# Attention scores as two products over all 128 rows, with tokens stored so that position classes are runs of 16 words

## The chip, the core and the metric

The kernel runs on one core of a Trainium2 chip. The core has five engines with instruction queues of their own: TensorE (PE, matrix products; its weight loads are listed apart as PEld), VectorE (DVE), ScalarE (ACT), GpSimd (POOL) and SyncE (SP, which here issues every DMA). The metric is the device time of one execution in microseconds (us); lower is better. The kernel before takes 2600.39 us, the median of 3 runs (2598.51 to 2601.74).

## What is computed

One encoder layer runs over two independent streams: a prompt of 1024 tokens and a sample of 512, 1024 channels each, all in float32. Per stream:

```
u = rmsnorm(x) @ w_in
ssd_out = ssd_mixer(...)                       # scan over chunks, both directions
att_out = attention_mixer(u_q, u_k, u_v, ...)  # 8 heads of 64 channels
h = x + concat(ssd_out, att_out) @ w_out
h = h + memory_cross_attention(rmsnorm(h), rmsnorm(mem), ...)
y = h + square(relu(rmsnorm(h) @ w1)) @ w2
```

The change is in `attention_mixer`. Queries and keys are normed and rotated, and then

```
for window, dil in ((128, 1), (512, 4), (2048, 16)):
    o, lse = band_pattern(q, k, v, dil, window // (2 * dil))
w = softmax(stack(lses)); out = sum(w * stack(outs))
```

Each pattern lets a query see the keys of its own class of positions modulo `dil`, at most 64 steps of that class away. All three together are one softmax over the union, with keys that are counted twice where two patterns hold them.

## The kernel before, in words

Precision. TensorE multiplies rounded float32 words (F32R). A number is split into a rounded part (hi) and the exact rest (lo), and a product of two such numbers is three products: hi·hi, hi·lo and lo·hi (`mm3`, L171 to L174). These are most of TensorE's work. Weights are loaded as `raw` by SP, rounded by ScalarE into `whi`, and the rest `wlo` is made by GpSimd or VectorE (`load_w`, L153 to L165; `raw` has two buffers).

Stages. The input projection writes its parts to DRAM: `heads` (L411 on) norms and rotates queries and keys, transposes them on TensorE (L423, with the unit matrix `ident`) and stores them as `qk`, rounded part and rest, tokens along the row. Values are stored as `vd` token by token (L442). The scan (`ssd`), the attention (`att`), the memory's keys and values, `w_out`, the cross attention and the MLP follow.

Attention. `att` runs `att_pair` for four pairs of heads. `att_load` (L575) loads a pair's operands: per head `aq` holds the rounded queries (64 rows) above their rests (64 rows), `ak` the rounded keys twice above each other, and `akl` the rests of both heads' keys. There is one buffer of each, so a pair waits for the pair before it. The work goes in units of two tiles of 128 queries of one head. First come the band units (neighbouring positions), then the class units (positions modulo 4, for the two dilated patterns). In a class unit the operands are read from the same tiles with a step of four: `q[:, r:T:4]` and `k[:, 64 + r:64 + T:4]`. The scores of one tile are two products into PSUM bank `ma`:

```
nc.tensor.matmul(pq[:, i, :W], q(qA[h]), k(kB[h]), start=True, stop=False)        # L638
nc.tensor.matmul(pq[:, i, :W], q(qA[h][rs]), k(kC[rs]), start=False, stop=True)   # L639
```

L638 goes over 128 rows (hi·hi + lo·hi) and L639 over the 64 rows of one head (hi·lo). W, the number of keys, is 256, and 128 in the class units of the sample. VectorE adds the mask and takes the maximum (L641), ScalarE takes the exponential (L646), TensorE transposes the result (L652, bank `mb`), VectorE or ScalarE copies it to `apT`, and TensorE multiplies it by the values (L662, bank `mc`; `avb` for the band, `avc` for classes). The results of a class unit go through DRAM (`ncl`) back into token order and are merged with those of the band. At the end `mix_T` (L753) loads both mixers' results and transposes them with `to_T` (L185).

The sample has 32 units (16 band, 16 class), the prompt 64 (32 and 32).

Order. The order of all instructions on each engine is made before the run by a scheduler that simulates the program's time; each engine then works through its list in that order. Products of the input projection, of the memory, of `w_out` and of the cross attention stand between the steps of an attention unit.

## Time and profile before

| what | value |
|---|---|
| median of 3 runs | 2600.39 us (2598.51 to 2601.74) |
| span of the profiled execution | 2603.1 us, the only time that the profile gives for that execution |
| TensorE busy | 2537.7 us, 97% |
| TensorE weight loads | 2328.8 us, 89% |
| VectorE busy | 1404.3 us, 54% |
| ScalarE busy | 954.7 us, 37% |
| GpSimd busy | 678.0 us, 26% |
| DMA | 269.36 MB, 103 GB/s on average |

A row of the timeline has the start of an instruction, how long it took, its engine and line, and what it wrote and read (the moving operand first, then the weights). TensorE's products are pipelined: their durations overlap, so what a product costs in a stream is the distance from its start to the next one's. "Idle before" is time in which the engine did nothing before an instruction, and the name behind it is what ended that time.

### The profile page before, as it was taken

What the parts mean: (1) busy time and instruction counts of PE and PEld (TensorE: products, weight loads), DVE (VectorE), ACT (ScalarE), POOL (GpSimd) and SP (SyncE); (2) the same over time, 40 slices, a digit from 0 to 9 for tenths busy, and PEclk for the clock granted to TensorE, in tenths of its full rate; (3) what the DMA queues carried; (4) which work ended last, traced back from release to release, by engine and by line L of the source; (5) the groups of instructions that cost most, each with busy time, mean ns of one, the idle gap of its engine ahead of it and who ended that gap; (6) DMA issues with size and microseconds to landing.
All of it is one profiled execution on the core that took longest, in us unless ns stands there. A gap on an engine that the chain in (4) does not pass through costs nothing.

```text
span 2603.1 us, 43137 instructions
## 1 busy us (share of the span) xinstructions
PE 2537.7 (97%) x17363; PEld 2328.8 (89%) x17363; DVE 1404.3 (54%) x2734; ACT 954.7 (37%) x2153; POOL 678.0 (26%) x476
## 2 busy tenths in 40 slices
PE   8989999899899999999999999999999999999999
PEld 8889999889888888788999999999899898999987
DVE  6895663787644454645544564544734434444344
ACT  5655443355544454443222232433522121212110
POOL 3362011565322121214333321111222122212211
PEclk9999999999999999989999999999999999999999
DMA  6755342656736242414322251111111111110101
GB/s 191 239 195 156 94 135 84 217 186 210 213 115 212 62 119 72 125 37 168 99 95 96 83 172 39 42 57 49 49 33 50 49 49 49 49 49 33 65 33 65
DMA packets 216054, 269.36 MB, mean 103 GB/s; under 512 B 26514, under 2 KB 171184, under 8 KB 215856
## 3 DMA queue, kind: packets, MB, share of 16 engines
q1 hardware_dynamic: 215856, 266.62, 32.1%
q8 instruction: 136, 2.23, 0.4%
q14 instruction: 62, 0.51, 0.1%
HBM read 212.37 MB, written 54.20 MB: 102 GB/s over the span
## 4 chain that ended last, share of the span: by engine, by line
PE 71%; DVE 4%; DMA 2%; ACT 1%; issue 1%; POOL 1%; SPq 0%; DVEq 0%; POOLq 0%; ACTq 0%
PE mm L172 13%; PE mm L174 13%; PE mm L173 13%; PE tp L174 7%; PE tp L173 7%; PE tp L172 7%; PE mc L662 2%; PE ma L639 2%; PE ma L638 2%; PE mb L652 1%; PE tp L190 1%; DMA se<-acp 1%; DVE wlo L164 1%; DVE se L545 1%; PE tp L801 0%
## 5 line engine op out<-in xcount | busy, mean ns | idle before, releaser
L172 PE MATMUL mm<-whi,chi 128*128 128x256 f32 x1792 | 517.6, 289 | 3.9 <-DVE h L779 2.0
L174 PE MATMUL mm<-whi,clo 128*128 128x256 f32 x1792 | 514.1, 289 | 2.3 <-DVE clo L196 2.3
L173 PE MATMUL mm<-wlo,chi 128*128 128x256 f32 x1792 | 514.3, 288 | 0.0
L926 DVE TENSOR_TENSOR h<-mm,h 128x512 f32<-128x512 f32 x384 | 261.9, 689 | 422.5 <-PE mm L174 422.5
L164 POOL TENSOR_TENSOR wlo<-raw,whi 128x1024 fp32r<-128x1024 f32 x120 | 294.2, 2452 | 697.7 <-ACT whi L163 693.4
L174 PE MATMUL tp<-chi,wlo 128*128 128x256 f32 x1440 | 409.3, 284 | 0.0
L173 PE MATMUL tp<-clo,whi 128*128 128x256 f32 x1440 | 408.4, 284 | 0.0
L172 PE MATMUL tp<-chi,whi 128*128 128x256 f32 x1440 | 406.1, 282 | 0.0
L163 ACT CAST whi<-raw 128x1024 fp32r<-128x1024 f32 x240 | 241.9, 1047 | 338.1 <-PE mm L174 208.6
L172 PEld LDWEIGHTS mm<-whi,chi 128*128 128x128 f32 x1792 | 342.6, 191 | 8.6 <-ACT mm L729 2.3
L173 PEld LDWEIGHTS mm<-wlo,chi 128*128 128x128 f32 x1792 | 342.4, 191 | 2.9 <-issue 0.9
L174 PEld LDWEIGHTS mm<-whi,clo 128*128 128x128 f32 x1792 | 340.8, 191 | 4.7 <-DVE clo L196 2.5
L164 DVE TENSOR_TENSOR wlo<-raw,whi 128x1024 fp32r<-128x1024 f32 x120 | 270.3, 2252 | 102.9 <-ACT whi L163 98.1
L172 PE MATMUL mm<-whi,hidh 128*128 128x512 f32 x768 | 303.1, 395 | 1.2 <-DVE h L926 1.2
L173 PE MATMUL mm<-wlo,hidh 128*128 128x512 f32 x768 | 302.5, 394 | 0.0
L174 PE MATMUL mm<-whi,hidl 128*128 128x512 f32 x768 | 302.0, 393 | 0.0
L172 PEld LDWEIGHTS tp<-chi,whi 128*128 128x128 f32 x1440 | 273.4, 190 | 9.4 <-issue 0.4
L174 PEld LDWEIGHTS tp<-chi,wlo 128*128 128x128 f32 x1440 | 272.5, 189 | 7.2
L173 PEld LDWEIGHTS tp<-clo,whi 128*128 128x128 f32 x1440 | 271.6, 189 | 6.6
L911 POOL TENSOR_TENSOR hidl<-hr,hidh 128x512 fp32r<-128x512 f32 x96 | 136.4, 1420 | 453.4 <-ACT hidh L910 453.4
L910 ACT CAST hidh<-hr 128x512 fp32r<-128x512 f32 x96 | 59.6, 621 | 326.4 <-PE mm L173 249.9
L174 PEld LDWEIGHTS mm<-whi,hidl 128*128 128x128 f32 x768 | 144.3, 188 | 33.6
(282 smaller groups left out, 4550.7 us busy)
## 6 DMA issues: line engine op xcount, KB each, us to landing
raw<-in_mlp_w_dram SPq DMA_DIRECT2D x128, 512.0 KB, 4.2
raw<-in_w_in_dram SPq DMA_DIRECT2D x48, 512.0 KB, 4.8
qkp<-ev SPq DMA_DIRECT2D x32, 256.0 KB, 3.1
se<-acp SPq DMA_DIRECT2D x16, 512.0 KB, 5.0
raw<-in_xatt_wkv_dram SPq DMA_DIRECT2D x16, 512.0 KB, 4.4
raw<-in_w_out_dram SPq DMA_DIRECT2D x16, 512.0 KB, 4.6
raw<-in_xatt_wq_dram SPq DMA_DIRECT2D x16, 512.0 KB, 4.6
raw<-in_xatt_wo_dram SPq DMA_DIRECT2D x16, 512.0 KB, 3.8
```

The costliest lines, as they stand in the source:

```text
L163: nc.scalar.copy(hi[:, sl, :], raw)
L164: (nc.vector if s else nc.gpsimd).tensor_tensor(lo[:, sl, :], raw, f(hi[:, sl, :]), op=OP.subtract)
L172: nc.tensor.matmul(ps, lh, rh, start=start, stop=False)
L173: nc.tensor.matmul(ps, lh, rl, start=False, stop=False)
L174: nc.tensor.matmul(ps, ll, rh, start=False, stop=stop)
L190: nc.tensor.transpose(pt[:, k, t, :], xn[t][:, (2 * kp + k) * 128:(2 * kp + k + 1) * 128], ident)
L638: nc.tensor.matmul(pq[:, i, :W], q(qA[h]), k(kB[h]), start=True, stop=False)
L639: nc.tensor.matmul(pq[:, i, :W], q(qA[h][rs]), k(kC[rs]), start=False, stop=True)
L662: nc.tensor.matmul(po[:, i * 64:i * 64 + 64], pT[:, i * nk + j, :], ops[i][2][j][:, rs], start=j == 0, stop=j == nk - 1)
L910: nc.scalar.copy(hh[:, ft], r)
L911: nc.gpsimd.tensor_tensor(hl[:, ft], r, f(hh[:, ft]), op=OP.subtract)
L926: nc.vector.tensor_tensor(h[t][:, cs], ps, h[t][:, cs], op=OP.add)
```

## The change

Tokens are stored in another order. Within each group of 64 tokens, the 16 of class 0 (modulo 4) come first, then those of class 1, 2 and 3. For queries and keys a permutation matrix `perm` takes the place of the unit matrix in the transpose of `heads`; values are stored in that order by four DMAs in place of one; the masks of the band are permuted likewise; and `mix_T` turns the attention's half of the channels back by transposing with `back`. A class is then read from the keys as runs of 16 words, and a class's queries are copied into a tile of their own (`qc`) by GpSimd.

`att_load` is split: `att_values` loads the values of a pair, and `att_head` the queries and keys of one head. Both key tiles now have the same keys in both halves: `k[0]` the rounded part twice, `k[1]` the rest twice. A tile's scores are two products over 128 rows with the same queries: (hi + lo)·hi and (hi + lo)·lo, so lo·lo is added to what was computed. A head's band units and class units come one after the other, then the second head. Keys and queries have three buffers each, and a head takes two of each.

```diff
@@ tables, constants
-T_BAND, T_CLP, T_CLS, T_ROPE = 256, 256 + 768, 256 + 768 + 512, 256 + 768 + 512 + 128
-T_END = T_ROPE + 128
+T_BAND, T_CLP, T_ROPE = 256, 256 + 704, 256 + 704 + 512
+T_PERM, T_BACK = T_ROPE + 128, T_ROPE + 256
+T_END = T_BACK + 128
...
+    tok = np.arange(64).reshape(16, 4).T.reshape(-1)
+    tok = (64 * np.arange(4)[:, None] + tok).reshape(-1)
+    t[tok[:128], T_PERM + np.arange(128)] = 1.0
+    t[np.arange(128), T_BACK + tok[:128]] = 1.0
...
+    perm, back = tab[:, T_PERM:T_PERM + 128], tab[:, T_BACK:T_BACK + 128]
@@ to_T
-                    nc.tensor.transpose(pt[:, k, t, :], xn[t][:, (2 * kp + k) * 128:(2 * kp + k + 1) * 128], ident)
+                    nc.tensor.transpose(pt[:, k, t, :], xn[t][:, (2 * kp + k) * 128:(2 * kp + k + 1) * 128],
+                                        units(2 * kp + k))
@@ heads, w_in_qkv
-                    nc.tensor.transpose(pt[:, o:o + 128], e[:, i, hp * 128:hp * 128 + 128], ident)
+                    nc.tensor.transpose(pt[:, o:o + 128], e[:, i, hp * 128:hp * 128 + 128], perm)
...
-                    dst = st.vd[64 + t * 128:64 + t * 128 + 256, (c - 4) * 256:(c - 3) * 256]
-                    nc.sync.dma_start(dst.rearrange("(t p) c -> p t c", p=128), e)
+                    for i in range(2):
+                        for g in range(2):
+                            r0 = 64 + (t + i) * 128 + g * 64
+                            dst = st.vd[r0:r0 + 64, (c - 4) * 256:(c - 3) * 256]
+                            nc.sync.dma_start(dst.rearrange("(r j) c -> j r c", r=4), e[g * 64:g * 64 + 64, i, :])
@@ att_load becomes att_values and att_head
-        qA = [pool.tile([128, T], F32R, name=f"aq{h}", bufs=1) for h in range(2)]
-        kB = [pool.tile([128, T + 128], F32R, name=f"ak{h}", bufs=1) for h in range(2)]
-        kC = pool.tile([128, T + 128], F32R, name="akl", bufs=1)
...
-        for h in range(2):
-            a, o = half[h], half[1 - h]
-            nc.sync.dma_start(f(qA[h])[a], qh[a])
-            nc.sync.dma_start(f(kB[h])[a, ks], kh[a])
-            nc.sync.dma_start(f(kB[h])[o, ks], kh[a])
-            nc.sync.dma_start(f(qA[h])[o], ql[a])
-        nc.sync.dma_start(f(kC)[:, ks], kl)
...
-        src = st.vd[64:64 + T, c0:c0 + 128].rearrange("(a p r) c -> p r a c", r=4, p=128)
-        for r in range(4):
-            nc.sync.dma_start(vc[:, r], src[:, r])
-        return vb, vc, qA, kB, kC
+        for a in range(nt // 4):
+            src = st.vd[64 + a * 512:64 + a * 512 + 512, c0:c0 + 128].rearrange("(g r j) c -> r g j c", r=4, j=16)
+            for r in range(4):
+                nc.sync.dma_start(vc[:, r, a], src[r])
+        return vb, vc
+
+    def att_head(st, pool, hp, h):
+        T = st.T
+        k = [pool.tile([128, T + 128], F32R, name="ak", bufs=3) for _ in range(2)]
+        q = pool.tile([128, T], F32R, name="aq", bufs=3)
+        a, o = (slice(h * 64, h * 64 + 64), slice(64 - h * 64, 128 - h * 64))
+        for j in range(2):
+            nc.vector.memset(f(k[j])[:, 0:64], 0.0)
+            nc.vector.memset(f(k[j])[:, T + 64:T + 128], 0.0)
+            nc.sync.dma_start(f(q)[(a, o)[j]], st.qk[0, hp, j][a])
+            for b in (a, o):
+                nc.sync.dma_start(f(k[j])[b, 64:T + 64], st.qk[1, hp, j][a])
+        qc = pool.tile([128, T], F32R, name="aq", bufs=3)
+        nc.gpsimd.tensor_copy(qc.rearrange("p (r g j) -> p r g j", r=4, j=16),
+                              f(q).rearrange("p (g r j) -> p r g j", r=4, j=16))
+        return (q, qc), k
@@ att_pair
-                return (lambda q: q[:, r:T:4][:, a * 128:a * 128 + 128], lambda k: k[:, 64 + r:64 + T:4],
-                        [vc[:, r, j] for j in range(na)], tab[:, c:c + W])
+                return ([k[:, 64:64 + T].rearrange("p (g r j) -> p r g j", r=4, j=16)[:, r] for k in ks],
+                        [vc[:, r, j] for j in range(na)], tab[:, c:c + W])
...
-                        nc.tensor.matmul(pq[:, i, :W], q(qA[h]), k(kB[h]), start=True, stop=False)
-                        nc.tensor.matmul(pq[:, i, :W], q(qA[h][rs]), k(kC[rs]), start=False, stop=True)
+                    qu = q[:, (u0 + i) * 128:(u0 + i) * 128 + 128]
+                    for j in range(2):
+                        nc.tensor.matmul(pq[:, i, :W], qu, ops[i][0][j], start=j == 0, stop=j == 1)
...
-                    out = order(st.ncl)[:, u // na, u % na, :]
-                    nc.sync.dma_start(out[:, hp * 132:hp * 132 + 132], no[:, i].rearrange("p h e -> p (h e)"))
+                    out = st.ncl[a0:a0 + 512, c0:c0 + 66].rearrange("(g r j) c -> r g j c", r=4, j=16)
+                    nc.sync.dma_start(out[r], no[:, i])
+
+        for h in range(2):
+            qs, ks = att_head(st, pool, hp, h)
+            for classes in (False, True):
+                part(h, classes, qs, ks)
@@ mix_T
-        to_T(xs, *st.mixT[-1], lambda k: gcol("ssd_norm_g", k), banks)
+        to_T(xs, *st.mixT[-1], lambda k: gcol("ssd_norm_g", k), banks,
+             lambda k: ident if k < 4 else back)
```

What the scheduler makes of it on TensorE, first in the kernel before: two band units of the prompt's first pair, one for each head. `ma` is the bank of the scores, `ak` and `akl` are keys, `aq` queries, `mm` a bank of the projections.

```order
L174 MATMUL mm<-whi,clo 128x256
L638 MATMUL ma<-ak_8112,aq_8110 128x256
L639 MATMUL ma<-akl,aq_8110 128x256
L638 MATMUL ma<-ak_8112,aq_8110 128x256
L639 MATMUL ma<-akl,aq_8110 128x256
L662 MATMUL mc<-avb,apT 128x64 x4
L652 MATMUL mb<-ident,asc 128x128 x4
L638 MATMUL ma<-ak_8113,aq_8111 128x256
L639 MATMUL ma<-akl,aq_8111 128x256
L638 MATMUL ma<-ak_8113,aq_8111 128x256
L639 MATMUL ma<-akl,aq_8111 128x256
L172 MATMUL mm<-whi,chi 128x256
```

And the same place in the kernel after, where a band unit is L653 and the projection's products are L181 to L183.

```order
L183 MATMUL mm<-whi,clo 128x256
L676 MATMUL mc<-avb,apT 128x64 x4
L666 MATMUL mb<-ident,asc 128x128 x4
L653 MATMUL ma<-ak,aq 128x256 x4
L181 MATMUL mm<-whi,chi 128x256
L182 MATMUL mm<-wlo,chi 128x256
L183 MATMUL mm<-whi,clo 128x256
```

The two lines that took turns, one over 128 and one over 64 rows, have become one line that comes four times, all over 128 rows. What stands before and behind a unit is of the same kinds.

On TensorE in the kernel after, with the numbers of the buffers, this is where the prompt's first pair goes from its first head (keys 8222 and 8223) to its second (keys 8449 and 8450). The first piece is the last score unit of the first head, the second piece the first products of the second head; 45 products and transposes (some rows hold two or four) stand between the last product with 8222 and the first with 8450, which takes over the buffer of 8222.

```order
L653 MATMUL ma_8422<-ak_8222,aq_8235 128x256
L653 MATMUL ma_8422<-ak_8223,aq_8235 128x256
L653 MATMUL ma_8422<-ak_8222,aq_8235 128x256
L653 MATMUL ma_8422<-ak_8223,aq_8235 128x256
L181 MATMUL mm_11106<-whi_11068,chi_7980 128x256
...
L676 MATMUL mc_8413<-avc_8212,apT_8411 128x64 x4
L653 MATMUL ma_8464<-ak_8449,aq_8451 128x256
L181 MATMUL mm_11140<-whi_11068,chi_8038 128x256
L182 MATMUL mm_11140<-wlo_11069,chi_8038 128x256
L653 MATMUL ma_8464<-ak_8450,aq_8451 128x256
L653 MATMUL ma_8464<-ak_8449,aq_8451 128x256
L666 MATMUL mb_8434<-ident_73,asc_8423 128x128 x2
```

In the kernel before, both heads' keys are there from the start of the pair, and nothing is handed over at this point.

On SP, the loads that belong to that place, in the kernel after:

```order
L683 DMA nclp_106<-ano_8365 8x16x66 x2
L614 DMA ak_8450<-qkp_103 64x1024 x2
L612 DMA aq_8712<-qkp_103 64x1024
L614 DMA ak_8710<-qkp_103 64x1024 x2
L612 DMA aq_8712<-qkp_103 64x1024
L755 DMA vs_98<-ev_11132 128x512
L171 DMA raw_11545<-in_w_out_dram 128x4x256
L755 DMA vs_98<-ev_11133 128x512
L683 DMA nclp_106<-ano_8393 8x16x66 x2
L171 DMA raw_11549<-in_w_out_dram 128x4x256
```

The second load group of `ak_8450` waits for the first head's last score product. Behind it on SP are the queries and the first keys of the next pair's first head, stores of the memory's values, and weights (`raw`) of the filler. In the kernel before, a pair's nine loads stand together:

```order
L592 DMA aq0_8572<-qkp_103 64x1024
L593 DMA ak0_8574<-qkp_103 64x1024
L594 DMA ak0_8574<-qkp_103 64x1024
L595 DMA aq0_8572<-qkp_103 64x1024
L735 DMA vp_110<-ev_10988 128x512
L735 DMA vp_110<-ev_10989 128x512
L593 DMA ak1_8575<-qkp_103 64x1024
L592 DMA aq1_8573<-qkp_103 64x1024
L594 DMA ak1_8575<-qkp_103 64x1024
L595 DMA aq1_8573<-qkp_103 64x1024
L596 DMA akl_8576<-qkp_103 128x1024
L162 DMA raw_11455<-in_w_out_dram 128x4x256
```

They come once per pair, ahead of the weights of the filler, where after there are two groups of loads per pair.

## Rows read from the trace of the kernel before

**Rows 1.** The page: busy us (share of the span) and instructions of each engine.

```profile
PE 2537.7 (97%) x17363; PEld 2328.8 (89%) x17363; DVE 1404.3 (54%) x2734; ACT 954.7 (37%) x2153; POOL 678.0 (26%) x476
```

**Rows 2.** Busy time by stages: window, its length, each engine, granted clock, DMA share, GB/s.

```profile
205.00:442.00 237.00, 235.60 (x1752) 219.20 (x1750) 134.37 (x394) 113.44 (x298) 28.63 (x17) 1.00 0.38 114
...
697.00:1176.00 479.00, 462.57 (x2967) 404.82 (x2966) 231.48 (x638) 214.74 (x604) 87.12 (x55) 0.95 0.37 112
1176.00:2600.00 1424.00, 1421.27 (x9387) 1300.38 (x9385) 671.33 (x940) 380.50 (x676) 331.21 (x200) 1.00 0.20 67
```

**Rows 3.** Timeline of TensorE, a band unit: start, duration, engine, line, operation.

```profile
714.07 0.28 PE L172 MATMUL mm<-whi,chi 128*128 128x256 f32 x1
...
714.54 0.28 PE L638 MATMUL ma<-ak,aq 128*128 128x256 f32 x1
714.75 0.38 PE L639 MATMUL ma<-akl,aq 64*128 64x256 f32 x1
715.06 0.39 PE L638 MATMUL ma<-ak,aq 128*128 128x256 f32 x1
715.38 0.38 PE L639 MATMUL ma<-akl,aq 64*128 64x256 f32 x1
715.69 0.38 PE L173 MATMUL mm<-wlo,chi 128*128 128x256 f32 x1
715.91 0.28 PE L174 MATMUL mm<-whi,clo 128*128 128x256 f32 x1
```

**Rows 4.** Timeline of the weight loads at the same unit.

```profile
714.31 0.19 PEld L172 LDWEIGHTS mm<-whi,chi 128*128 128x128 f32 x1
714.43 0.19 PEld L638 LDWEIGHTS ma<-ak,aq 128*128 128x128 f32 x1
714.75 0.18 PEld L639 LDWEIGHTS ma<-akl,aq 64*128 64x128 f32 x1
```

**Rows 5.** Timeline of TensorE, a class unit of the prompt.

```profile
781.47 0.49 PE L638 MATMUL ma<-ak,aq 128*128 128x256 f32 x1
781.89 0.59 PE L639 MATMUL ma<-akl,aq 64*128 64x256 f32 x1
782.42 0.60 PE L638 MATMUL ma<-ak,aq 128*128 128x256 f32 x1
...
783.70 0.28 PE L172 MATMUL mm<-whi,chi 128*128 128x256 f32 x1
```

**Rows 6.** Timeline of TensorE, a class unit of the sample.

```profile
318.83 0.37 PE L638 MATMUL ma<-ak,aq 128*128 128x128 f32 x1
...
320.59 0.28 PE L172 MATMUL mm<-chi,whi 128*128 128x256 f32 x1
```

**Rows 7.** Who waited for the scores' second product, us and times.

```profile
  DVE asc L641: 102.8, 68
```

**Rows 8.** Waits of TensorE: us in total, times, longest us.

```profile
PE ma L638 <- DMA aq<-qkp: 3.9, 1, 3.9
...
PE mm L174 <- POOL wlo L164: 0.4, 1, 0.4
...
PE ma L638 <- DVE aband L641: 0.3, 1, 0.3
```

**Rows 9.** Busy time in a stretch of the prompt's attention.

```profile
715.00:780.00 65.00, 65.00 (x438) 57.19 (x437) 29.02 (x81) 28.39 (x85) 14.13 (x9) 0.97 0.35 118
```

**Rows 10.** Loads of keys: durations of the issue in ns, and us to landing.

```profile
L594 SPq DMA_DIRECT2D ak<-qkp x8: 587/590/1185, 694.8 to 1044.8; - x8
...
DMA to landing us min/median/max: 2.4/3.7/8.8
```

**Rows 11.** The page's costliest groups: GpSimd's part of the weight rests.

```profile
L164 POOL TENSOR_TENSOR wlo<-raw,whi 128x1024 fp32r<-128x1024 f32 x120 | 294.2, 2452 | 697.7 <-ACT whi L163 693.4
```

**Rows 12.** DMA issues: KB each, median us to landing.

```profile
ak<-qkp SPq DMA_DIRECT2D x16, 256.0 KB, 4.7
...
ak<-qks SPq DMA_DIRECT2D x16, 128.0 KB, 2.8
```

More of the change, by code (lines that the diff above doesn't have):

```diff
@@ L38, in tables @@
     t[:, T_TB:T_TB + 128] = p >= i
+    j, pq = tok[None, :], tok[:128, None]
+    band = (j - pq >= 0) & (j - pq <= 128)
+    for o, ok in ((0, band), (256, band & (j < 192)), (448, band & (j >= 64))):
+        t[:, T_BAND + o:T_BAND + o + 256] = np.where(ok, 0.0, NEG)
     j = np.arange(256)[None, :]
-    band = (j - p >= 0) & (j - p <= 128)
-    for v, ok in enumerate((band & (j >= 64), band, band & (j < 192))):
-        t[:, T_BAND + 256 * v:T_BAND + 256 * v + 256] = np.where(ok, 0.0, NEG)
     def count(mq, mk):
@@ L609, in att_pair, with part @@
         na = T // 512
-        vb, vc, qA, kB, kC = att_load(st, pool, hp)
+        vb, vc = att_values(st, pool, hp)
         band = pool.tile([128, nt, 2, 66], F32, name="aband", bufs=1)
-        order = lambda ap: ap.rearrange("(a p r) c -> p r a c", r=4, p=128)
-        for classes in (False, True):
+        def part(h, classes, qs, ks):
+            rs = slice(h * 64, h * 64 + 64)
             W = 128 if classes and na == 1 else 256
             nk = W // 128
+            q = qs[classes]
             def operands(u):
@@ L623, in operands @@
                 r, a = u // na, u % na
-                c = T_CLS if na == 1 else T_CLP + 256 * a
-                return (lambda q: q[:, r:T:4][:, a * 128:a * 128 + 128], lambda k: k[:, 64 + r:64 + T:4],
+                c = T_CLP + 256 * a
+                return ([k[:, 64:64 + T].rearrange("p (g r j) -> p r g j", r=4, j=16)[:, r] for k in ks],
                         [vc[:, r, j] for j in range(na)], tab[:, c:c + W])
             for u0 in range(0, nt, 2):
-                no = band[:, u0:u0 + 2] if not classes else pool.tile([128, 2, 2, 66], F32, name="ano", bufs=2)
@@ L665, in att_pair @@
-                for i in range(2 if classes else 0):
-                    u = u0 + i
-                    out = order(st.ncl)[:, u // na, u % na, :]
-                    nc.sync.dma_start(out[:, hp * 132:hp * 132 + 132], no[:, i].rearrange("p h e -> p (h e)"))
+                no = pool.tile([128, 2, 66], F32, name="ano", bufs=2) if classes else band[:, u0:u0 + 2, h]
+                ops = [operands(u0 + i) for i in range(2)]
+                pq = mx_bank("a").rearrange("p (u k) -> p u k", u=2)
@@ new lines, in part @@
+                sc = pool.tile([128, 2, 256], F32, name="asc", bufs=2)
+                mx = pool.tile([128, 2], F32, name="amx", bufs=4)
+                for i in range(2):
+                    qu = q[:, (u0 + i) * 128:(u0 + i) * 128 + 128]
+                    for j in range(2):
+                        nc.tensor.matmul(pq[:, i, :W], qu, ops[i][0][j], start=j == 0, stop=j == 1)
+                for i in range(2):
+                    nc.vector.tensor_tensor_reduce(out=sc[:, i, :W], in0=pq[:, i, :W], in1=ops[i][2],
+                                                   scale=1.0, scalar=-3e38, op0=OP.add, op1=OP.max,
+                                                   accum_out=no[:, i, 65:66])
@@ new lines, in part @@
+                nc.vector.tensor_scalar(mx, no[:, :, 65], -0.125, None, op0=OP.mult)
+                for i in range(2):
+                    nc.scalar.activation(sc[:, i, :W], sc[:, i, :W], AF.Exp, scale=0.125, bias=mx[:, i:i + 1],
+                                         accum_out=no[:, i, 64:65])
+                pt = mx_bank("b")
+                for i in range(2):
+                    for j in range(nk):
+                        o = (i * nk + j) * 128
+                        nc.tensor.transpose(pt[:, o:o + 128], sc[:, i, j * 128:j * 128 + 128], ident)
@@ new lines, in part @@
+                pT = pool.tile([128, 4, 128], F32, name="apT", bufs=2)
+                pTf = pT.rearrange("p a b -> p (a b)")
+                if u0 % 4:
+                    nc.scalar.copy(pTf[:, :2 * W], pt[:, :2 * W])
+                else:
+                    nc.vector.tensor_copy(pTf[:, :2 * W], pt[:, :2 * W])
+                po = mx_bank("c")
+                for i in range(2):
+                    for j in range(nk):
+                        nc.tensor.matmul(po[:, i * 64:i * 64 + 64], pT[:, i * nk + j, :], ops[i][1][j][:, rs],
+                                         start=j == 0, stop=j == nk - 1)
```

56 lines of the change are left out of this document (9 added, 47 removed).

## The prediction

> **What bounds the kernel now.** I read the busy shares first. TensorE is busy for 97% of the span, VectorE for 54%, ScalarE for 37% and GpSimd for 26% [rows 1]. Then the stages. The change touches two of them: the attention of the sample stream, mixed with other work from about 205 to 442 us, and that of the prompt stream, from about 697 to 1176 us. In these TensorE is busy for 235.6 of 237 us and for 462.6 of 479 us, while VectorE is busy for about half of each [rows 2]. After 1176 us it is busy for 1421 of 1424 us, without any attention scores. So a microsecond of TensorE time taken out of the attention is a microsecond off the end, as long as nothing new makes TensorE wait: the scheduler fills between the attention's steps with projection products, and what is not used there as filler is done later at full rate.
>
> Third, the timeline of TensorE around the scores, read by starts and not by durations, since the durations overlap. An ordinary product of 256 columns starts 0.118 us after the one before: four of them from 714.07 to 714.54 [rows 3]. The four score products of a band unit (two tiles of 128 queries, two products each) start 0.21, 0.31, 0.32 and 0.31 us apart, and the projection product behind them still takes 0.22 us [rows 3]. The weight loads say why: an ordinary load starts 0.12 us after the one before and lies under the running product, but the load of L639 (64 rows) starts together with its own product at 714.75, not ahead of it [rows 4]. The switch between a 128-row and a 64-row product, in either direction, takes the cover from a load of 0.19 us. In a class unit of the prompt the first product takes 0.42 us and the second 0.53 us [rows 5], and the two after it are like the second. They have the same switches, and on top of them operands read with a step of four words.
>
> **The change, part by part.** Score products stay 384 (96 units of four), and each is now 128 rows against 128 rows.
>
> Band units: 48 (16 of the sample, 32 of the prompt). Before, the four products and the one behind them take 715.91 − 714.54 = 1.37 us [rows 3]. Five ordinary starts take 5 × 0.118 = 0.59 us. Gain 0.78 us, times 48: 37.4 us.
>
> Class units of the prompt: 32. Before, 783.70 − 781.47 = 2.23 us [rows 5]; after, with contiguous queries and keys in runs of 16 words, I take the ordinary 0.59 us. Gain 1.64 us, times 32: 52.5 us. Of each unit's gain 0.78 us is the switch and 0.86 us the step. If runs of 16 words were still read at the price of a step of four, the product itself would keep its part: 0.53 − 0.31 us is the step's price in the spacing, about half of it the moving side (0.11 us a product, an estimate: a 256-column product at half speed). I take nothing, the row of contiguous products, because 15 of 16 words follow their neighbour.
>
> Class units of the sample: 16, of 128 columns. Before, 320.59 − 318.83 = 1.76 us [rows 6]. After, a 128-column product with its load costs between 0.06 us (half of 0.118) and 0.118 us; no row shows one between ordinary loads, and loads stand 0.12 us apart [rows 4], so I take 0.118. Gain 1.76 − 0.59 = 1.17 us, times 16: 18.7 us (up to 4 us more at the other end).
>
> Sum on TensorE: 37.4 + 52.5 + 18.7 = 108.6 us.
>
> Is the chain behind the scores late next? VectorE's maxima waited 102.8 us for the second product, in 68 waits [rows 7], so they begin earlier by themselves when the scores end earlier, and TensorE waited 0.3 us in all for one of the attention's VectorE steps and never for its ScalarE steps [rows 8]. The cover stays, shorter by what the scores shrink.
>
> The clock: over the prompt's attention the granted share is 0.95 [rows 2], that is about 2 × 0.05 × 479 = 48 us at the lower level (1.2 GHz in place of 2.4), which cost about 24 us. From 715 to 780 us it is 0.97 though TensorE never idles [rows 9], so some of these drops follow stretches of scores with little streaming in them and not waits. Those might go. Bounds 0 and 24 us; most drops in this stretch I can't tie to the scores, so I take 5.
>
> What is added. By the order of instructions SP issues 124 more DMAs (764 to 888): 24 for queries and keys, 48 for class results in pieces of 264 bytes, 36 for values stored, 16 for values loaded. At 0.59 us an issue [rows 10] that is 73 us of SP over some 970 us, in which it is far from full; it costs nothing where nothing late stands behind it. GpSimd gets 16 copies of a head's queries, each between 0 and the 2.45 us of a two-operand operation of 1024 columns [rows 11], at most 39 us on an engine at 26%, and TensorE waited 0.4 us in all for GpSimd's weight rests [rows 8]: hidden. 16 small memsets on VectorE are within its waits. The transposes by a permutation in place of the unit matrix are as many and as large as before: nothing, with bounds of a few us either way.
>
> The one added wait that can be seen is the hand-over from head to head. Keys have three buffers and a head takes two, so the second key tile of a later head is loaded only when the previous head's last score product is done: 14 times, 7 in each stream. Its two issues and the landing take 0.59 + 2.8 = 3.4 us in the sample and 0.59 + 4.7 = 5.3 us in the prompt, an issue and a median landing each time [rows 10, 12]. In the new order the first product with that tile stands 38 TensorE instructions or more later in the sample and 34 to 50 later in the prompt (46 at the place shown ahead), which is 4.5 us and 4.0 to 5.9 us at 0.118 us each. So the sample is covered and the prompt is just so; a landing of 8.8 us, the longest [rows 10], would show up to 5 us. Behind the waiting DMA on SP stand the next head's queries and keys and the weights of the filler. Before, such a hand-over came once per pair (8 of them), and TensorE waited 3.9 us for it, once [rows 8]. Bounds 0 and 14 × 5 = 70 us; the rows of before stand nearer to the lower end, and there are more hand-overs now: I take 8.
>
> Two rules of the Trainium skill stand against this reckoning. "TensorE: Matmul & The Clock Gate", section "The mechanism", says that a weight load overlaps a running product only where the row group differs; by it four 128-row products in a row would hide no load, which is the second rival below. The trace doesn't agree for ordinary products: their loads of 0.19 us start every 0.12 us under products of the same 128 rows [rows 4]. "SBUF — State Buffer", section "Door 1: The DMA port swizzle", gives lines of 16 bytes and says that fp32 can be stepped by four for free; by it the classes would cost what the band costs, and what they cost more would not be the step's and would stay (the first rival below). The rows differ here too (0.53 against 0.31 us a product [rows 3, 5]), and the measurement decides.
>
> Total: 2603.1 − 108.6 − 5 + 8 = 2497.5 us against the profiled span of 2603.1 us. The median of the runs, 2600.4, is 2.7 us below that span, so the forecast is 2495 us.
>
> **The rivals.**
> The classes stay dear. If only the moving side does, in runs of 16, it keeps 0.11 us on 128 products of the prompt and half of that on 64 of the sample: 14 + 3.5 us, time 2512 us. If all of their extra price stays, since something else than the step makes it, the gain is 96 × 0.78 = 75 us and the time 2529 us. For it: the rows show only steps of four and contiguous words. Against it: queries become contiguous, and keys nearly so.
>
> Loads of the same rows don't overlap. Each score product would keep its 0.19 us load in front, as the second one of a band unit does now. Band units gain nothing, the prompt's classes fall to the band's price (2.23 − 1.37 = 0.86 us, 27.5 us) and the sample's by about 0.5 us (8 us). With the same clock and waits as above (−5, +8) the time is 2600 − 36 + 3 = 2567 us. Rows 4 speak against it. This is also the case in which the change doesn't do what it says, though its products are all of 128 rows.
>
> Hand-overs show. If landings are as slow as in a busy stretch, or the shorter scores uncover waits that they hid, 14 hand-overs at some 2.7 us more: 38 us. Time 2533 us. For it: the cover in the prompt is even with the need.
>
> Slower: SP stands at the second key tile until the head before is done, and the weights of the filler queue behind it, so that TensorE has neither scores nor filler. To cancel the gain each of 14 hand-overs has to cost 105 / 14 = 7.5 us more; at 9 us it is 2495 + 126 = 2621 us. Against it: 8 such hand-overs cost 3.9 us in all before, and the weights have two buffers as loaded and three as split.
>
> **How the numbers follow.** Forecast 0.66 (2475 to 2515: clock 0 to 24 us, waits 0 to 20). The classes stay dear 0.10 (0.07 in the moving side alone). Loads don't overlap 0.06. Hand-overs show 0.12. Slower 0.04. The rest, 0.02, is no change within 0.2% (about what a measurement of this kernel can tell from none). The range of 2470 to 2535 us holds the first two cases and the fourth; outside are the other 0.12 and the edges of those. Faster 0.94, same 0.02, slower 0.04.
>
> **What the profile after would show.** Score products at 0.118 us from start to start, in band and class alike, and loads ahead of them: the switch and the step are right. Class products still at 0.2 us: the first rival. 0.31 us everywhere: the second. TensorE's busy time should fall to about 2430 us with its idle time near the 65 us of now; more than 25 us on top, on keys or on weights after the end of a head, would make the hand-over the story. The granted share from 697 us on should be 0.95 or above.

## The result, and the profile after

The changed kernel takes 2491.55 us (median of four runs, 2489.01 to 2495.59) against 2601.06 us (2598.51 to 2604.59) for the kernel before: a ratio of 0.9586, with a 95% interval of 0.957 to 0.9602. That is 109.5 us less; the forecast was 2495 us.

The busy row of the profiled execution after (engine, busy us, share of the span, instructions), whose span is 2487.2 us, answers to [rows 1]:

```profile
PE 2419.2 (97%) x17363; PEld 2268.0 (91%) x17363; DVE 1394.9 (56%) x2750; ACT 951.3 (38%) x2153; POOL 698.4 (28%) x492
```

The span fell by 115.9 us, TensorE's busy time by 118.5 us (from 2537.7), with the same 17,363 products. Span less busy went from 65.4 to 68.0 us. So all of the gain is time in which TensorE worked, and next to nothing was given back as waits. Of the busy time some 14 us are the clock's (below); the rest, 104 us, is the products'.

The stages of the kernel after (window, length, busy time of PE, PEld, DVE, ACT and POOL, granted clock, DMA share, GB/s), to be laid beside [rows 2]:

```profile
205.00:442.00 237.00, 234.36 (x2002) 232.20 (x2001) 153.78 (x438) 124.37 (x322) 49.57 (x38) 1.00 0.44 131
697.00:1176.00 479.00, 466.60 (x3530) 442.50 (x3531) 279.15 (x699) 235.72 (x618) 136.64 (x80) 0.99 0.46 138
1176.00:2485.00 1309.00, 1304.93 (x8641) 1194.83 (x8639) 608.81 (x864) 346.65 (x627) 285.76 (x178) 1.00 0.18 61
```

In the same stretches of time TensorE starts 250 products more (2002 for 1752) in the sample's attention, and 563 more (3530 for 2967) in the prompt's. It doesn't finish the attention and stop; the scheduler brings projection products of later stages forward, and the stage behind 1176 us is shorter by 115 us. That is why a microsecond saved in the scores was one at the end, far from it. The granted share in the prompt's attention rose from 0.95 to 0.99.

Now the score products themselves. TensorE's timeline after (start, duration, line, operation; "x4" is four instructions merged into one row), a unit of 256-column products among projection products, answers to [rows 3] and [rows 5]:

```profile
851.43 0.36 PE L183 MATMUL mm<-whi,clo 128*128 128x256 f32 x1
851.63 0.64 PE L653 MATMUL ma<-ak,aq 128*128 128x256 f32 x4
852.10 0.28 PE L181 MATMUL mm<-whi,chi 128*128 128x256 f32 x1
852.22 0.27 PE L182 MATMUL mm<-wlo,chi 128*128 128x256 f32 x1
```

Its weight loads, answering to [rows 4]:

```profile
851.40 0.19 PEld L183 LDWEIGHTS mm<-whi,clo 128*128 128x128 f32 x1
851.51 0.55 PEld L653 LDWEIGHTS ma<-ak,aq 128*128 128x128 f32 x4
851.99 0.19 PEld L181 LDWEIGHTS mm<-whi,chi 128*128 128x128 f32 x1
```

Four score products and the one behind them take 852.22 − 851.63 = 0.59 us, five times 0.118. The four loads start at 851.51, 0.12 us ahead of the first product, and the next line's load at 851.99 starts under the fourth: cover is back, between loads that all use 128 rows. A class unit of the prompt behind transposes, and one of the sample (128 columns), the same view; they answer to [rows 5, 6]:

```profile
713.00 0.61 PE L666 MATMUL mb<-ident,asc 128*128 128x128 f32 x4
713.36 0.73 PE L653 MATMUL ma<-ak,aq 128*128 128x256 f32 x4
713.93 0.28 PE L182 MATMUL mm<-wlo,chi 128*128 128x256 f32 x1
714.04 0.28 PE L183 MATMUL mm<-whi,clo 128*128 128x256 f32 x1
...
300.70 0.56 PE L653 MATMUL ma<-ak,aq 128*128 128x128 f32 x4
301.10 0.33 PE L182 MATMUL mm<-clo,whi 128*128 128x256 f32 x1
301.26 0.28 PE L183 MATMUL mm<-chi,wlo 128*128 128x256 f32 x1
```

The prompt's unit takes 714.04 − 713.36 = 0.68 us, with a first product of 0.20 us behind a transpose. That is also the median of the prompt's class units, most of which stand behind a transpose or a product with values (median before, counted alike: 2.30 us); behind an ordinary product it is 0.61 us (2.21 before). The sample's takes 301.26 − 300.70 = 0.56 us (1.76 before). The 0.08 us behind a transpose are paid before as after, so they drop out of the gain.

What TensorE waited for around the attention (engine, tile, line, releaser: us in total, times, longest), beside [rows 8]; the first row is of the kernel before, the others of the kernel after:

```profile
PE tp L423 <- DVE ev L418: 17.0, 9, 3.3
```

```profile
PE tp L433 <- DVE ev L428: 11.9, 7, 3.2
...
PE ma L653 <- DMA ak<-qkp: 5.4, 3, 2.8
...
PE ma L653 <- DVE aband L655: 4.3, 4, 2.7
...
PE ma L653 <- DMA aq<-qkp: 2.5, 1, 2.5
```

Key tiles now cost 5.4 us where they cost nothing, and VectorE's band maxima 4.3 us where they cost 0.3; queries went from 3.9 to 2.5 us, and what the transposes in `heads` wait for the normed and rotated queries and keys of both streams went from 17.0 to 11.9 us. VectorE's own wait for the scores, 102.8 us in 68 waits [rows 7], is now

```profile
DVE asc L655 <- PE ma L653: 43.7, 27, 7.7
```

### The profile page after: what moved, and what is told of

The parts are those of the page before. It is cut to its first block, busy times and chain, and to the rows that moved or that the text cites. A ratio compares the mean times of both kernels' runs of the same rounds, so it can differ in the third digit from the quotient of the medians.

```text
span 2487.2 us, 43450 instructions
## 1 busy us (share of the span) xinstructions
PE 2419.2 (97%) x17363; PEld 2268.0 (91%) x17363; DVE 1394.9 (56%) x2750; ACT 951.3 (38%) x2153; POOL 698.4 (28%) x492
## 4 chain that ended last, share of the span: by engine, by line
PE 79%; DMA 6%; DVE 6%; issue 3%; POOL 2%; ACT 2%; SPq 1%; POOLq 0%; DVEq 0%; ACTq 0%
PE mm L181 16%; PE mm L183 16%; PE mm L182 16%; PE tp L183 7%; PE tp L182 7%; PE tp L181 7%; PE mc L676 2%; PE ma L653 2%; PE mb L666 1%; DMA se<-acp 1%; DVE wlo L173 1%; PE tp L199 1%; DVE se L558 1%; POOL wlo L173 1%; DMA ak<-qkp 1%
## 5 line engine op out<-in xcount | busy, mean ns | idle before, releaser
L181 PE MATMUL mm<-whi,chi 128*128 128x256 f32 x1792 | 516.6, 289 | 2.1 <-ACT mm L749 1.2
L183 PE MATMUL mm<-whi,clo 128*128 128x256 f32 x1792 | 512.2, 287 | 0.0
L183 PE MATMUL tp<-chi,wlo 128*128 128x256 f32 x1440 | 408.4, 284 | 0.0
L181 PE MATMUL tp<-chi,whi 128*128 128x256 f32 x1440 | 405.6, 282 | 0.0
L181 PEld LDWEIGHTS mm<-whi,chi 128*128 128x128 f32 x1792 | 341.1, 190 | 4.5 <-ACT chi L205 1.7
L183 PEld LDWEIGHTS mm<-whi,clo 128*128 128x128 f32 x1792 | 339.9, 190 | 0.4
L181 PE MATMUL mm<-whi,hidh 128*128 128x512 f32 x768 | 303.1, 395 | 0.2 <-DVE h L947 0.2
L183 PE MATMUL mm<-whi,hidl 128*128 128x512 f32 x768 | 302.3, 394 | 0.2 <-POOL hidl L932 0.2
L181 PEld LDWEIGHTS tp<-chi,whi 128*128 128x128 f32 x1440 | 272.5, 189 | 8.7
L183 PEld LDWEIGHTS tp<-chi,wlo 128*128 128x128 f32 x1440 | 271.7, 189 | 7.0
L183 PEld LDWEIGHTS mm<-whi,hidl 128*128 128x128 f32 x768 | 144.3, 188 | 34.0 <-POOL hidl L932 0.6
```

The costliest lines, as they stand in the source:

```text
L181: nc.tensor.matmul(ps, lh, rh, start=start, stop=False)
L183: nc.tensor.matmul(ps, ll, rh, start=False, stop=stop)
```

## The experiments

All ratios are to the kernel before, run on the same chip beside the kernel named. A difference between two kernels that did not run side by side is taken from their ratios, times 2600 us.

**The row count alone, undone (rows64).** The kernel after, with the second product of each pair over the head's 64 rows again; layout, order of heads and all transfers stay.

```
-    nc.tensor.matmul(pq[:, i, :W], qu, ops[i][0][j], ...)
+    rr = rs if j else slice(0, 128)
+    nc.tensor.matmul(pq[:, i, :W], qu[rr], ops[i][0][j][rr], ...)
```

> The kernel after, but the second score product goes over the 64 rows of its head again (so low queries times low keys are left out, as before). Token order, copies, loads and buffers stay. Theory (the switch between 128-row and 64-row products uncovers weight loads): every unit of four goes from 0.59 us back to about 1.37 us, band and class alike, so 96 x 0.78 = 75 us more: 2566 us, and the loads of the 64-row products start together with their products. Rival (the step of four made the price, rows hardly count): 2491 us within 0.5%.

Measured: 2557.4 us, 0.9836 (0.9819 to 0.9853), 65 us above the kernel after; TensorE's busy time is 2491.5 us, 72.3 more. Its timeline, a band unit:

```profile
343.37 1.22 PE L654 MATMUL ma<-ak,aq 128*128 128x256 f32 x4
344.51 0.39 PE L183 MATMUL mm<-chi,wlo 128*128 128x256 f32 x1
344.74 0.27 PE L181 MATMUL mm<-chi,whi 128*128 128x256 f32 x1
```

and the load of the product behind it:

```profile
344.51 0.19 PEld L183 LDWEIGHTS mm<-chi,wlo 128*128 128x128 f32 x1
```

The unit is back at 1.37 us, to the hundredth what it was before, and the load at 344.51 starts together with its own product: its cover is gone. The prompt's class units are at 1.47 us in the median and the sample's at 1.14. The switch between row counts is shown as the cause of some 0.8 us a unit of 256 columns; with 128 columns it costs 0.57 us, so that the sum is 48 × 0.78 + 32 × (1.47 − 0.68) + 16 × 0.57 = 72 us, as the busy time says. The profiled span grew by 68.3 us, as span less busy fell by 4.0.

**The row count alone, done (before128).** The kernel before, with its low halves of the keys stored twice above each other, once per head, so that both products have 128 rows; operands keep their step of four words.

```
-    nc.tensor.matmul(pq[:, i, :W], q(qA[h][rs]), k(kC[rs]), ...)
+    nc.tensor.matmul(pq[:, i, :W], q(qA[h]), k(kC[h]), ...)
```

> The kernel before, with the rests of each head's keys loaded twice above each other, so that the second score product goes over 128 rows too (low times low is added). Token order and the step of four stay. Theory: band units fall to 0.59 us (37 us less); class units lose the switch and keep the step, with the load of 0.31 us now under the running product: about 0.95 to 1.35 us in the prompt, 0.7 to 1.3 in the sample (35 to 57 us less). Together 2507 to 2529 us, a few less if the granted clock drops less often. Rival (a stepped load can't lie under a product): class units stay near 2.2 us and the time is about 2563 us.

Measured: 2515.22 us, 0.9678 (0.9662 to 0.9694). Timeline of a class unit of the prompt, then its loads:

```profile
734.53 0.58 PE L640 MATMUL ma<-ak,aq 128*128 128x256 f32 x1
734.92 0.42 PE L641 MATMUL ma<-akl,aq 128*128 128x256 f32 x1
735.16 0.42 PE L640 MATMUL ma<-ak,aq 128*128 128x256 f32 x1
735.40 0.42 PE L641 MATMUL ma<-akl,aq 128*128 128x256 f32 x1
735.63 0.30 PE L173 MATMUL mm<-wlo,chi 128*128 128x256 f32 x1
735.77 0.28 PE L174 MATMUL mm<-whi,clo 128*128 128x256 f32 x1
```

```profile
734.71 0.33 PEld L641 LDWEIGHTS ma<-akl,aq 128*128 128x128 f32 x1
734.95 0.33 PEld L640 LDWEIGHTS ma<-ak,aq 128*128 128x128 f32 x1
```

The products stand 0.24 us apart, twice the ordinary 0.118, and the loads take 0.33 us in place of 0.19. But each load starts 0.24 us after the one before and lies under the running product. The unit is 735.77 − 734.53 = 1.24 us, not the 0.59 + 0.86 = 1.45 that the prediction's split would leave: about a quarter of the 0.86 us went with the switch. So the two halves of the change aren't separate.

That the slower load is covered here doesn't make it free. The sample's class units in the same kernel have products of 128 columns; two of them, and their loads:

```profile
239.08 0.42 PE L641 MATMUL ma<-akl,aq 128*128 128x128 f32 x1
239.32 0.42 PE L640 MATMUL ma<-ak,aq 128*128 128x128 f32 x1
...
238.99 0.33 PEld L641 LDWEIGHTS ma<-akl,aq 128*128 128x128 f32 x1
239.22 0.33 PEld L640 LDWEIGHTS ma<-ak,aq 128*128 128x128 f32 x1
```

They too stand 0.23 to 0.24 us apart, with half of the columns. In runs1 below, the same products with the same step on the moving side and ordinary loads stand 0.118 us apart. So loads with a step come one in 0.23 us by themselves, as fast as 256 stepped columns are streamed. In the prompt's units the two costs are equal and lie over each other, and which of them sets the pace can't be told there; the first, uncovered load of a unit still shows, as the unit is 0.11 us longer than in runs1. Equal rows without the new order bring 82 us (2597.66 − 2515.22), the whole change 24 us more.

**The step of the moving side alone (runs1).** The kernel after with tokens in their own order: a class is every fourth word of the keys, the queries stay contiguous per class, and the values' stores and the gathers follow.

```
-    tok = np.arange(64).reshape(16, 4).T.reshape(-1)
-    tok = (64 * np.arange(4)[:, None] + tok).reshape(-1)
+    tok = np.arange(4).reshape(1, 4).T.reshape(-1)
+    tok = (4 * np.arange(64)[:, None] + tok).reshape(-1)
```

> The kernel after with runs of one word: tokens in their own order, so a class's keys are read with a step of four, while its queries are still copied into a contiguous tile and both products go over 128 rows. Only the moving side has the step. Theory (the moving side is read at half speed): class units of the prompt 0.59 + 4 x 0.107 = 1.0 us, of the sample about 0.8 us, 14 + 3 us more: 2508 us. Rival one (the step cost only in the weight load): 2491 us. Rival two (all of the step's 0.86 us is the moving side's): 2491 + 34 = 2525 us.

Measured: 2511.2 us, 0.9663 (0.9647 to 0.9678), 20 us above the kernel after; busy time 23.7 us more. A class unit of the prompt:

```profile
964.94 1.17 PE L650 MATMUL ma<-ak,aq 128*128 128x256 f32 x4
965.92 0.32 PE L181 MATMUL mm<-whi,chi 128*128 128x256 f32 x1
966.07 0.28 PE L182 MATMUL mm<-wlo,chi 128*128 128x256 f32 x1
```

The unit is 1.13 us, its products 0.233 us apart. The load is ordinary here, so this is the moving side alone: half speed. The sample's units, of 128 columns, are at 0.595 us and hardly show it. Behind a transpose both times, the prompt's units make 32 × (1.13 − 0.68) = 14 us of the 20. The rest isn't the step's alone: this kernel stores its values by 12 DMAs, and the kernel after with that change only (12stores, below) is 8 us slower too.

**Where full speed begins (runs4, then st96_runs4 and st96_runs2).** Runs of 4 words in place of 16 first, as groups of 16 tokens; the values, whose stores put their rows in class order, take 192 DMAs this way in place of 48.

```
-    tok = np.arange(64).reshape(16, 4).T.reshape(-1)
+    tok = np.arange(16).reshape(4, 4).T.reshape(-1)
...
-    for g in range(2):
+    for g in range(8):
```

> The kernel after with runs of 4 words (16 bytes) in place of 16. If a run of four words is read at full speed, class units stay at 0.59 us and the time at 2491 us within 0.3%. If every break of a run costs a word's time, 64 breaks in 256 columns add 0.027 us a product: class units 0.70 us, 4 us more. If runs shorter than 16 are read like a step of four, about 1.0 us a class unit: 2508 us.

Measured: 2577.15 us, 0.9921 (0.9904 to 0.9937), 87 us above the kernel after by the ratios. A class unit of the prompt, however:

```profile
965.44 0.72 PE L653 MATMUL ma<-ak,aq 128*128 128x256 f32 x4
966.00 0.38 PE L822 MATMUL tp<-ident,xq 128*128 128x128 f32 x2
```

The four products take 0.56 us behind a transpose, as those at 713.36 above do with 0.57: full speed. The time went elsewhere. The stretch from 585 to 715 us of this kernel, and the value stores in it (durations in ns: least, median, most):

```profile
585.00:715.00 130.00, 107.61 (x729) 99.10 (x729) 80.84 (x180) 57.41 (x165) 48.83 (x44) 0.86 0.47 147
...
L456 SPq DMA_DIRECT2D vdp<-ev x128: 582/582/675, 588.0 to 703.7; - x128
```

and the same two rows of the kernel after:

```profile
585.00:715.00 130.00, 115.71 (x892) 111.48 (x891) 83.14 (x201) 71.37 (x205) 57.84 (x44) 0.96 0.63 200
...
L456 SPq DMA_DIRECT2D vdp<-ev x12: 517/537/587, 588.2 to 610.8; - x12
```

SP spends 128 × 0.582 = 74 of 130 us on issuing these stores, in place of 6, and TensorE is busy for 108 us at a granted share of 0.86, where it was 116 us at 0.96. The DMA engines are busy for a smaller share there than in the kernel after (0.47 for 0.63), so it isn't they that are full. Over the whole span the granted share is 0.975 for 0.993: the lower clock takes away (1 − share) × span, 64 us in place of 17, and is more than half of the loss. To hold run length and stores apart, the stores were written class by class (96 DMAs whatever the run length), for runs of 16, 4 and 2 words:

```
-    for g in range(2):
-        ...
-        nc.sync.dma_start(dst.rearrange("(r j) c -> j r c", r=4), e[g * 64:g * 64 + 64, i, :])
+    for r in range(4):
+        nc.sync.dma_start(dst[r], e[r:128:4, i, :])
```

> The kernel after (runs of 16) with the values stored by 96 DMAs in place of 48, class by class. Nothing else changes. Theory (in the kernel with runs of 4 it was the 192 value stores, which kept SP issuing for 76 to 80% of the stretch from 585 to 715 us, and not the run length): more SP time costs, between 0 and 28 us (a third of that kernel's 86 us), 2491 to 2520 us. Rival (SP's count is free): 2491 us within 0.2%.

> Runs of 4 words with the values stored by 96 DMAs, as many as in the run with 96 stores and runs of 16. Theory (the run length of 4 is free, the stores cost): the same time as that run within 0.5%, and class units as long. Rival (runs of 4 are what cost): about 2570 us, as with 192 stores.

> Runs of 2 words with 96 value stores, beside the runs of 4 and of 16 with as many. If two words in a row are enough for full speed, class units are as long as with runs of 4 (0.67 us behind a transpose) and the time is 2510 to 2522 us. If they are read like a step of four, class units take about 1.1 us, 15 us more.

Measured: runs of 16 words 2522.06 us, 0.9695 (0.9682 to 0.9709); runs of 4 words 2512.55 us, 0.9657 (0.9641 to 0.9672); runs of 2 words 2530.82 us, 0.9734 (0.972 to 0.9748). A class unit of 4 words, then one of 2:

```profile
1066.38 0.72 PE L654 MATMUL ma<-ak,aq 128*128 128x256 f32 x4
1066.94 0.28 PE L182 MATMUL tp<-clo,whi 128*128 128x256 f32 x1
1067.05 0.28 PE L183 MATMUL tp<-chi,wlo 128*128 128x256 f32 x1
```

```profile
886.53 1.17 PE L654 MATMUL ma<-ak,aq 128*128 128x256 f32 x4
887.50 0.31 PE L183 MATMUL mm<-whi,clo 128*128 128x256 f32 x1
887.65 0.28 PE L181 MATMUL mm<-whi,chi 128*128 128x256 f32 x1
```

Both stand behind a transpose: 0.67 against 1.12 us. Runs of 4 words are as fast as runs of 16, and runs of 2 as slow as single words; between 4 and 2 the time differs by 20 us, of which the prompt's class units make 32 × 0.45 = 14. And 192 stores against 96 at the same runs of 4 cost 0.9921 − 0.9657, 69 us: in runs4 the stores, not the runs, made the loss. Why 96 stores cost 28 us more than 48 at runs of 16 isn't settled, nor why runs of 4 with 96 stores are 10 us under runs of 16 with as many. The clock has a part in both: in the profiled executions the granted share is 0.985 with runs of 16 and 0.989 with runs of 4 (37 and 28 us taken away), for 0.993 with 48 stores (17 us). SP's time doesn't order them: one of these stores takes it 0.48 us with runs of 16 and 0.57 with runs of 4 (medians). Nor is the price a straight line in their number, as the next runs show.

**Fewer stores, or stores from another queue (12stores, actstores).** In the first, the permutation of the values is left out, and they are stored in token order by 12 DMAs. In the second, ScalarE issues the 48.

```
-    nc.sync.dma_start(dst.rearrange("(r j) c -> j r c", r=4), e[g * 64:g * 64 + 64, i, :])
+    nc.sync.dma_start(dst.rearrange("(t p) c -> p t c", p=128), e)
```

```
-    nc.sync.dma_start(dst.rearrange("(r j) c -> j r c", r=4), ...)
+    nc.scalar.dma_start(dst.rearrange("(r j) c -> j r c", r=4), ...)
```

> The kernel after with the values stored in token order by 12 DMAs, as before, so values don't stand in the order of the keys: the permutation of the values is left out, and nothing else. It prices the 36 added stores. Theory (SP's issue time): 0 to 21 us less (0.6 us a store, from 48 to 96 stores), 2470 to 2491 us. Rival (the first 36 were free, only more than these cost): 2491 us within 0.2%.

> The kernel after with its 48 value stores issued by ScalarE's queue and not by SP; the transfers are the same. Theory (it is SP's time to issue that made 96 stores cost 30 us): SP is relieved of 48 issues, 0 to 28 us less, 2463 to 2490 us; I expect about 2480. Rival (the transfers cost, wherever they are issued): 2491 us within 0.2%.

Measured: 12 stores 2499.42 us, 0.9617 (0.9603 to 0.963); on ScalarE's queue 2492.38 us, 0.9596 (0.9581 to 0.9611). Neither gains. So the 36 stores that the change added cost nothing that shows, as predicted. That 12 are 8 us slower than 48 is a miss for every theory; the products are the same, the order that the scheduler makes of them isn't, and busy time is 10.8 us more. Most of that is the clock: a granted share of 0.990 for 0.993 is some 8 us. What in the order makes it fall stays open.

**The hand-over from head to head (keys2, keys4, keys4_act).** Two buffers for keys in place of three, so that each head's first tile waits for the head before as well; then four, with the queries in two sets of one buffer to make room; then four, and the stores of values and class results on ScalarE's queue too.

```
-    k = [pool.tile([128, T + 128], F32R, name="ak", bufs=3) for _ in range(2)]
+    k = [pool.tile([128, T + 128], F32R, name="ak", bufs=2) for _ in range(2)]
```

```
-    k = [pool.tile([128, T + 128], F32R, name="ak", bufs=3) for _ in range(2)]
-    q = pool.tile([128, T], F32R, name="aq", bufs=3)
+    k = [pool.tile([128, T + 128], F32R, name="ak", bufs=4) for _ in range(2)]
+    q = pool.tile([128, T], F32R, name="aq", bufs=1)
...
-    qc = pool.tile([128, T], F32R, name="aq", bufs=3)
+    qc = pool.tile([128, T], F32R, name="aqc", bufs=1)
```

> The kernel after with two key buffers: both key tiles of a head are loaded only when the head before is done, a need of about 4 x 0.59 + 4.7 = 7 us in the prompt and 5 us in the sample at each hand-over. Theory (the scheduler puts filler there and some of the need shows): 5 to 25 us more, 2497 to 2517 us. Rival (the prediction's slow case: weights queue behind the waiting loads and TensorE starves): 14 x 5 us and more, 2560 us or above.

> The kernel after with four key buffers in place of three, and one buffer each for a head's queries and for their copy in place of three in all. Both key tiles of the next head can then be loaded while the head before is worked on. Theory (the hand-over still costs what TensorE waits for keys and queries in the profile after, 5.7 + 2.5 us): 5 to 8 us less, 2484 to 2487 us, and no wait of TensorE for keys. Rival (other waits take its place): 2491 us within 0.15%.

> Four key buffers, and both the value stores (48) and the stores of class results (96) issued by ScalarE's queue. Theory (SP's issue time costs, and ScalarE at 38% has room for some 80 us): below the kernel with four key buffers (2487 us) by as much as the value stores alone bring and a little more, 2455 to 2480 us. Rival (ScalarE stands behind the attention's exponentials and copies, and its issues delay them): above 2490 us.

Measured: two buffers 2510.15 us, 0.9644 (0.9626 to 0.9662); four 2487.52 us, 0.9564 (0.9551 to 0.9578); four with ScalarE's stores 2505.34 us, 0.9649 (0.9634 to 0.9664). TensorE's waits for the prompt's keys with two buffers, then with four:

```profile
PE ma L653 <- DMA ak<-qkp: 6.4, 8, 1.8
```

```profile
PE ma L653 <- DMA ak<-qkp: 1.6, 1, 1.6
```

Two buffers cost 15 us by the ratios, though the prompt's keys are waited for only 6.4 us in all: span less busy rose by 12.6 us to 80.6, most of it at other lines, which were not followed. With four the waits for keys fall from 5.4 to 1.6 us and span less busy from 68.0 to 61.0 us. Its time is the lowest measured, 6 us under the kernel after by the ratios, but the intervals overlap: a gain over the kernel after isn't shown. What the hand-over still costs after the change is then some 7 us at most. On ScalarE's queue the stores made it worse by 22 us; that engine's own work stands behind them, but which wait did it was not followed.

## Why the prediction was right

**The score units, −108.6 us.** Predicted 0.59 us a unit of each kind; measured 0.59 (band), 0.61 (class of the prompt) and 0.56 (class of the sample), each behind an ordinary product. The gains of a unit are right, the sum is a little high. From start to next start, waits taken out, all 384 score products take 147.2 us in the trace of before and 50.7 in that of after, and the ordinary products behind them 7 us less: 103 us, or some 106 if the other products behind units gain as much. The band units are short, 33 to 35 us for 37.4; 19 of the 96 units are broken up by other products after, 11 before. rows64 and before128 show the switch, runs1 the step, each undone or done by itself. The reading by starts held: the durations of the products, 0.28 us in [rows 3] and now, say nothing of the gain.

**Its split was too simple.** The prediction gave 0.78 us of a class unit to the switch and 0.86 us to the step, as if they added up. before128 shows that a part of the stepped load's price went with the switch already: equal rows put it under the prompt's products, which stood 0.24 us apart by then. For the whole change that makes no difference; for either half alone it does. The estimate of the moving side at half speed, 0.11 us a product, was right (0.233 − 0.118).

**Runs of 16 words read at full speed.** This was taken on the ground that 15 of 16 words follow their neighbour. The value was right and the ground too weak: runs of 2, in which half of the words do, gained nothing, and runs of 4 all.

**The two rules weighed.** Loads of the same rows are covered: those from 851.51 on are, 0.12 us apart. The Trainium skill, "TensorE: Matmul & The Clock Gate", section "The mechanism", says in one sentence that a load overlaps only where the row group differs, which this trace contradicts, and in another that a load into the background weight buffer is pulled ahead too, which it doesn't. Single words with a step of four are read at half speed in runs1 (0.233 us a product), and so are runs of 2 words (0.233). The Trainium skill, "SBUF — State Buffer", section "Door 1: The DMA port swizzle", gives four fp32 as how far one can step for free, and the measurement decides against that; the prediction left out that the same passage puts a penalty on each access that crosses to a new line of 16 bytes, and by this a step of four is slow, as measured. It also says that two accesses to a line are enough for full speed; runs of 2 words, at half speed, don't bear that out. Runs that fill a line are read at full speed.

**The clock, −5 us.** In the profiled pair the mean granted share is 0.988 before and 0.993 after; time at the lower level takes away (1 − share) × span, 31 and 17 us, a gain of 14 us. But that pair flatters: the kernel before, in its 24 later runs, had 0.988 to 0.993 with the middle at 0.990, and the kernel after 0.991 to 0.993 with the middle at 0.992. That is 26 and 20 us, a gain of about 6 with an uncertainty of some 2 from the rounding. The term was right in size, and in the profiled pair its gain lies where it was expected, in the prompt's attention (0.95 to 0.99 of 479 us, 19 us).

**The waits, +8 us.** Keys, queries and band maxima cost 5.4 + 0.3 + 4.3 + 2.5 us after against 3.9 + 0.3 before, 8.3 us more; as other waits shrank, span less busy rose by 2.6 us only. keys2 shows that the mechanism is real and the third buffer hides most of it. SP's 124 more DMAs and GpSimd's copies cost nothing that shows, and one of the copies took 1.04 us at the median, inside the bounds given.

**The sum.** The predicted −108.6 − 5 + 8 is −105.6 us. What the traces give, −103 to −106 for the scores, −14 for the clock and 2.6 for the waits, is −114 to −117 us against −115.9 in the profiled pair; with the medians' clock, −6, it is −106 to −109 against −109.5. TensorE's busy time, expected at about 2430 us, is 2419, as the clock gave more in this pair. That the forecast lies within 4 us of the result is in part luck: the scores' gain was taken some 3 to 5 us too high and the waits about 5 us too high, and the two cancel. The mechanism and its size don't rest on that. None of the rivals came: no unit was at 0.31 us a product, classes stayed at the band's price, and SP never starved TensorE. runs4 shows what the slower rival would have looked like, a queue full of issues and TensorE short of work, at four times the stores.

## What to carry to other kernels

Give neighbouring products the same row count, even when half of the rows then have to be stored twice: it puts the weight loads back under the products, and that was 65 to 82 of these 109 us. Lay what is streamed as the moving side in runs of at least 4 fp32 words, and the stationary side without a step as well: stepped by four, its loads come one in 0.23 us, which is covered only under products that take as long. No run has a stepped load under 256 columns at full speed. When a layout is paid for in DMAs, count the issues on their queue by stretch: 48 cost nothing here, 192 most of the gain.

## What the runs showed of the hardware that was not expected

- A moving operand of fp32 has two speeds here, and none between in the four lengths tried: 0.118 to 0.123 us per 256 columns in runs of 4 and 16 words, 0.233 in runs of 1 and 2.
- A stationary operand with a step of four words loads in 0.31 to 0.34 us in place of 0.19, for 128 columns, and such loads start 0.23 to 0.24 us apart at best in before128, under products of 256 and of 128 columns alike; ordinary loads start 0.12 us apart.
- A store of values with a permuted pattern takes SP 0.48 to 0.59 us to issue at the median, where one in token order takes 0.37; 192 of them at 0.58 are over 100 us of a queue that weights use too. runs4 lost 69 us against 96 stores; that SP's time does it, and not something else about the stores, isn't shown by itself.
- A unit of 128-column products takes 0.56 us, one of 256 columns 0.59: half of the columns saves next to nothing. Loads of 0.19 us start 0.11 to 0.12 us apart under both. That they set the pace of the 128-column products is borne out by before128, where a slower load moves these from 0.12 to 0.23 us apart.
- The mean granted share of one and the same kernel wanders from 0.988 to 0.993 between its runs, and its time with it (2592 to 2605 us before). A pair of profiles can be off by 8 us for that reason alone, so the clock's part is read from several runs.
